# A new place in SBUF for the tiles of an MLP's second matrix, other pairs for the sums of its blocks, and one VectorE operation for the final scaling

## The chip, the cores and the metric

The kernel runs on one core of a Trainium2 chip. TensorE multiplies, VectorE, ScalarE and GpSimd work on vectors, and SyncE's queue issues nearly all DMA transfers. The metric is the device time of one execution in microseconds (us). An execution takes a little longer than the span of the profile, which runs from its first to its last instruction.

## The reference, cut to what matters

One step of a decoder layer for 1024 prompt tokens and 32 sample tokens (T = 1056 columns in all), with a width of 1024: attention and a short convolution, merged and projected, then an MLP and a last normalization. Everything is float32. The change touches the end alone:

```
h2 = rms_norm(x2, g_mlp)              # 1056 x 1024
u  = square(relu(h2 @ w_up))          # 1056 x 4096
x3 = x2 + u @ w_down                  # 1056 x 1024
y  = rms_norm(x3, g_final)
```

## The kernel before, in words

**Split products.** A float32 factor is split into a high part (a ScalarE cast to the matmul's reduced float32 type) and a low part (a VectorE subtraction), and each product is three matmuls (mm3: high by high, high by low, low by high; lines 216 to 218 of the profile). So each weight or activation tile costs a load, a cast and a subtraction before TensorE can use it.

**Strassen-like blocks.** Both matrix products of the MLP are cut into 2 x 2 blocks and done with seven block products in place of eight (Winograd's form). Each needs sums of blocks of the weights and of the activations.

**The stage of w_up** runs over 16 pairs p of column blocks of w_up. A pair is seven products, numbered 1 to 7 here: product 1 with hA[0], 2 with hA[1], then those with t2, t3, t1, t4 and b22, which are sums of blocks of h2. One product is 24 matmuls into one wide PSUM buffer (tile c); there are four such buffers. VectorE adds each product to what it belongs to, ScalarE applies the square of relu (put, line 1473), and SyncE stores the result u to DRAM (u_d, line 1478).

**The sums of w_down.** Between these products, VectorE also makes the sums of w_down's blocks, 16 blocks in all: load_sums loads two 512 KB pieces into a slot of tile h2r (line 1485), sums_down adds four times (lines 1492 to 1495) and stores 1 MB to DRAM (sd_d, line 1496). SDOWN says in which pair which block is done: block p - 1 in pair p, and blocks 14 and 15 both in pair 15. A pair's first block is put behind product 5, a second one behind product 7. There are four slots of h2r; three of them hold low parts of t1, t4 and b22 during the pairs, so one is free for the sums. Block 15 takes the slot of t1's low part, once product 5 of pair 15 has been done.

**The stage of w_down.** For n in (1, 2, 5, 6, 7, 4) it runs over 16 values of p. Each p takes a tile of activations (u_of: for n = 1 the tiles T0 to T15 are loaded from u_d, line 1567, and stay, since later n need them; for n = 2 tiles ur are loaded), and a weight block of 128 x 512 (wrd, line 1552, from w_down itself or from sd_d). Casts (lines 1554 for the weights, 1560 for the activations) and subtractions (1555 and 1561) make the split tiles whd and ud. Then come 96 matmuls into four PSUM buffers, one for each of four column blocks d. At the end of an n the four buffers are copied or added into accumulators acc. The product n = 3 follows, with calls of rows_out in it that finish rows which are complete, and a tail with the remaining rows (rows_out for row tiles 8, 6, 7; last for 4 and 5).

**The final scaling.** rows_out squares a row tile on ScalarE, adds on VectorE, takes the power -1/2 on GpSimd (factor, line 1670), and multiplies by that factor and by g_final: for the row tiles that start at the rows in YV with one VectorE operation (line 1683), for the others with ScalarE (1685) and then GpSimd (1686).

**Where tiles lie.** Pools are opened from the left and from the right end of SBUF. When the pools of w_up's stage close ("hB", "q", "w", "h2"), those of w_down's stage take their room, in the order in which they are opened. A new tile waits for the last readers of the old tiles under it (reuse_waits="tile"). Before, from the left, in bytes of a partition: ud [18112, 35008), where hA[0] was and a little of hA[1]; wd (the split weights) [35008, 51392), the rest of hA[1]; T [51392, 85184), over all four h2r slots, with T0 at the top, over the slot of b22's low part, which product 7 reads.

**The order.** The order of instructions on each engine and queue is set ahead of the run by the framework's scheduler, which plays the program through with estimates of its own (schedule_with_timeline_sim=True). On the chip each engine and queue goes through its list in that order and stops at an instruction whose semaphores aren't there yet.

Of the kernel before, what the change touches and what calls it, by code (L numbers as in the profile page):

```python
# [11 lines left out]
F32 = mybir.dt.float32  # L12
# [4 lines left out]
OP = mybir.AluOpType  # L17
# [8 lines left out]
T = SEQ + NB * ST  # L26
HC = T // 2
# [41 lines left out]
UG = 1  # L69
TORDER = (0, 1, 2, 3, 8, 4, 5, 6, 7)  # L70
NP0 = 4
SDOWN = {**{p: (p - 1,) for p in range(1, 15)}, 15: (14, 15)}
WUB = 6
YV = (384, 512)
CB = 2
SADV = [2] * 10
SSTEP = [0, 0, 0, 0, 0, 0, 6, 6, 6, 6, 6, 6, 6, 6, 6, 7]
# [46 lines left out]
def tile_hybrid_step(ctx, tc, xp, xs, cck, ccv, csk, csv, swk, swv, sconv, ptab, g_attn, w_in,  # L124
# [5 lines left out]
    PE, V, S, P, DMA = nc.tensor, nc.vector, nc.scalar, nc.gpsimd, nc.sync  # L130
# [3 lines left out]
    def open_pool(name, side, bufs=1, **kw):  # L134
        es = ExitStack()
        pools[name] = es
        kw.setdefault("reuse_waits", "tile")
        return es.enter_context(tc.tile_pool(name=name, bufs=bufs, side=side, **kw))

    def close(*names):  # L140
        for n in names:
            pools.pop(n).close()

    cp = open_pool("cp", "left")
# [47 lines left out]
    def tok_rows(tt):  # L192
        if tt < 8:
            return xp[0, tt * 128:(tt + 1) * 128, :], 128
        return xs.rearrange("b t d -> (b t) d"), 32
# [19 lines left out]
    def mm3(out, wh, wl, ah, al, first, last):  # L215
        PE.matmul(out, wh, ah, start=first, stop=False)  # L216
        PE.matmul(out, wh, al, start=False, stop=False)  # L217
        PE.matmul(out, wl, ah, start=False, stop=last)  # L218
# [44 lines left out]
    for tt in range(9):  # L263
        src, m = tok_rows(tt)
        xt = wp.tile([128, D], F32, name="wru", tag="wru", bufs=WB)
# [8 lines left out]
        rs = ap_.tile([128, 1], F32, name="rs", tag="rs")  # L274
# [41 lines left out]
    for br, (c0, n, kc) in enumerate(((C_KC, 384, 256), (C_VS, 408, 128))):  # L316
        whs = [load_qkv(c0, n, k, P) for k in range(KT)] if br else wq
        h9 = h9 if br else pack(qp, hTh, hTl, "h9")
        for tt in range(9):
# [9 lines left out]
            m = 128 if tt < 8 else 32  # L329
# [90 lines left out]
    for j in range(4):  # L420
# [9 lines left out]
        for e in range(2):  # L430
# [3 lines left out]
                            op0=OP.mult)  # L434
# [307 lines left out]
    class Unit:  # L742
# [54 lines left out]
        def factor(self, br, parts=1):  # L797
            if parts == 2:
                V.tensor_add(self.st[:, br, 2, :], self.st[:, br, 2, :], self.st[:, br, 3, :])
            V.reciprocal(self.st[:, br, 3, :], self.st[:, br, 2, :])  # L800
# [168 lines left out]
    for j in range(16):  # L969
        js = slice(j % 8 * 128, j % 8 * 128 + 128)  # L970
        c = (C_GA, C_GB)[j // 8] + j % 8 * 128
# [30 lines left out]
    up = open_pool("unit", "right", bufs=2)  # L1002
# [400 lines left out]
    def wide():  # L1403
        return bank["p"].tile([128, 2, 512], F32, name="c", tag="c", bufs=bank["tags"]["c"])
# [14 lines left out]
    def load_up(f):  # L1419
        raw = wp.tile([128, KT, 128], F32, name="wru", tag="wru", bufs=4)  # L1420
        DMA.dma_start(raw, w_up[0, :, f * 128:(f + 1) * 128].rearrange("(k p) c -> p k c", p=128))
        return raw[:, :4], raw[:, 4:]

    def halves(raw):
        h, l = (wp.tile([128, 4, 128], F32R, name="wu" + x, tag="wu" + x, bufs=WUB) for x in "hl")
        S.copy(h, raw)
        V.tensor_sub(l, raw, f32(h))
        return h, l

    def product(w, h):  # L1430

        c = wide()[:, :, :HC // 2]
        for k in range(4):
            for i in range(2):
                s = slice(i * HC // 2, (i + 1) * HC // 2)
                mm3(c[:, i], w[0][:, k], w[1][:, k], h[0][:, k, s], h[1][:, k, s], k == 0, k == 3)
        return c
# [42 lines left out]
    def load_sums(p):  # L1480

        w = h2p.tile([128, 4, HC], F32, name="h2r", tag="h2r", bufs=4)
        w = w.rearrange("p a b -> p (a b)")[:, :2 * D].rearrange("p (a b) -> p a b", a=2)
        for i in range(2):
            DMA.dma_start(w[:, i], w_dn[0, (p + 16 * i) * 128:(p + 16 * i + 1) * 128])
        return p, w
# [11 lines left out]
    for p in range(16):  # L1498
        sd = [load_sums(i) for i in SDOWN.get(p, ())]
        w11, w12 = load_up(p)  # L1500
# [19 lines left out]
        c = product(halves(s1), hB["t1"])  # L1520
# [16 lines left out]

    up = open_pool("ud", "left")  # L1540
    dp = open_pool("wd", "left")
    rp = open_pool("T", "left")
    wp = open_pool("w", "right")
    lp = open_pool("mlp", "right")
    accp = open_pool("acc", "right")
    accs = [accp.tile([128, 4, HC], F32, name=f"acc{i}") for i in range(4)]
    res = [rp.tile([128, HC], F32, name=f"T{p}") for p in reversed(range(16))][::-1]
    lows = [None] * 3

    def split_w(src, pool=dp, tag="whd", bufs=4):  # L1550
        raw = wp.tile([128, 512], F32, name="wrd", tag="wrd", bufs=4)
        DMA.dma_start(raw, src)
        h, l = (pool.tile([128, 512], F32R, name="whd", tag=tag + x, bufs=bufs) for x in "hl")
        S.copy(h, raw)  # L1554
        lows.append(V.tensor_sub(l, raw, f32(h)))  # L1555
        return h, l

    def split_u(raw, c0=0, c1=HC, pool=up, tag="ud", bufs=4):
        h, l = (pool.tile([128, c1 - c0], F32R, name="ud", tag=tag + x, bufs=bufs) for x in "hl")
        S.copy(h, raw[:, c0:c1])  # L1560
        V.tensor_sub(l, raw[:, c0:c1], f32(h))
        return h, l
# [10 lines left out]
    def u_of(n, p):  # L1573

        if n == 1:
            return load_u(p, 0, res[p])
        if n == 2:
            return load_u(p + 16, 0)
        raw = load_u(*{5: (p, 1), 6: (p + 16, 1), 7: (p, 0), 4: (p + 16, 0), 3: (p + 16, 1)}[n])
        if n != 3:  # L1580

            with tc.issue_after(lows[-2].ins):
                if n in (5, 6):
                    V.tensor_sub(res[p], raw, res[p])
                    return res[p]
                V.tensor_sub(raw, res[p], raw)
        return raw

    def w_of(n, p):
        return {1: down_w(0, p)[:, :512], 2: down_w(1, p)[:, :512], 4: down_w(1, p)[:, 512:], 5: sd_d[p, :, 1, 512:],  # L1590
                6: sd_d[p, :, 0, :512], 7: sd_d[p, :, 0, 512:], 3: sd_d[p, :, 1, :512]}[n]
# [3 lines left out]
    for n in (1, 2, 5, 6, 7, 4):  # L1595
        cs = [wide()[:, :, :HC // 2] for _ in range(4)]
        for p in range(16):
            u = u_of(n, p)
            wh, wl = split_w(w_of(n, p))
            uh, ul = split_u(u)  # L1600
            if n == 2:

                ws.append(split_w(w_of(3, p), lp, "w3", 16))
            for d in range(4):
                ds = slice(d * 128, d * 128 + 128)
                for i in range(2):
                    s = slice(i * HC // 2, (i + 1) * HC // 2)
                    mm3(cs[d][:, i], wh[:, ds], wl[:, ds], uh[:, s], ul[:, s], p == 0, p == 15)
            if p >= 4 and behind:
                V.tensor_add(*behind.pop(0))  # L1610
        for d, c in enumerate(cs):
            a0, a1, a2, a3 = (a[:, d].rearrange("p (i c) -> p i c", i=2) for a in accs)
            if n == 1:
                S.copy(a0, c)
            elif n == 2:
                V.tensor_add(a1, c, a0)
            elif n == 5:
                S.copy(a2, c)
            elif n == 4:
                V.tensor_sub(a0, a0, c)  # L1620
            else:
                V.tensor_add(a0, c, a0)
            if n in (6, 7):
                behind.append((a3 if n == 6 else a2, a0, a2))
    close("T", "wd")

# [2 lines left out]
    gf = op.tile([128, D], F32, name="gf", bufs=1)  # L1631
# [29 lines left out]
    def sums(n):  # L1661

        ss = op.tile([128, n + 1], F32, name=f"ss{n}", tag=f"ss{n}")
        P.memset(ss[:, n:], D * EPS)
        return ss
# [7 lines left out]
    def rows_out(tt):  # L1673
        t0, m = tt * 128, 128 if tt < 8 else 32
        xt = residual(tt)
        yt = op.tile([128, D], F32, name="yt", tag="yt")
        ss = sums(2)
        for q in range(2):
            h = slice(q * 512, q * 512 + 512)
            S.activation(yt[:m, h], xt[:m, h], AF.Square, accum_out=ss[:m, q:q + 1])  # L1680
        rs = factor(ss, m)
        if t0 in YV:
            V.scalar_tensor_tensor(yt[:m], xt[:m], rs[:m], gf[:m], op0=OP.mult, op1=OP.mult)
        else:
            S.mul(yt[:m], xt[:m], rs[:m])
            P.tensor_mul(yt[:m], yt[:m], gf[:m])
        DMA.dma_start(y_p[0, t0:t0 + m, :] if t0 < SEQ else y_s.rearrange("b t d -> (b t) d"), yt[:m])


# [35 lines left out]
    for tt in (8, 6, 7):  # L1725
        rows_out(tt)
    last(5, early[1])
    bank["e"].close()
    close("out", "ud", "acc", "mlp", "w", "cp")
_INS = ["x_prompt", "x_sample", "cache_cmp_k", "cache_cmp_v", "cache_slc_k", "cache_slc_v", "state_win_k",  # L1730
        "state_win_v", "state_conv", "page_table", "g_attn", "w_in", "cmp_pe_k", "cmp_w1_k", "cmp_w2_k",
        "cmp_pe_v", "cmp_w1_v", "cmp_w2_v", "conv_w", "conv_b", "w_nsa_out", "w_conv_out", "w_o", "g_mlp",
# [29 lines left out]
```

## Time and profile before

| | us |
|---|---|
| median of 3 runs | 1980.15 (1978.64 to 1980.93) |
| the profiled execution | 1979.56 |
| its span | 1977.8 |
| TensorE busy | 1917.4 |
| last product of w_up's stage ends | 1610.98 |
| first matmul of w_down's stage | 1626.40 |
| last two stores issued | 1973.83 to 1974.79 |

The profiled execution lies 0.6 us below the median, within the spread of the runs. Its mean granted TensorE clock is 0.987 of full speed. In the profile's lines, L1567 is line 1567 of the kernel, "c<-ud,whd" is the tile written and the tiles read, SPq is SyncE's queue of DMA issues, and PE, DVE, ACT and POOL are TensorE, VectorE, ScalarE and GpSimd. PEld is TensorE's loading of weights. "<-" behind an idle time names what ended it.

### The profile page before, as it was taken

The page shows a single profiled execution, that of the slowest core. Times are in us where ns is not written, and L with a number is a line of the kernel's source. Part 1 is how long each engine was busy: PE and PEld are TensorE (multiplying, and loading weights), DVE is VectorE, ACT ScalarE, POOL GpSimd, SP SyncE. Part 2 cuts the span into 40 slices and gives each one's busy share as a digit, 9 for nine tenths or more (in the row PEclk, how much of TensorE's full clock was granted, in tenths as well). Part 3 has the DMA queues.
Part 4 walks back from the last instruction along what each step waited for, and adds up shares of the span by engine and source line. Part 5 has one row for each costly group of instructions (what it writes and reads, how often), then busy time and mean ns, then how long its engine had stood idle before and what let it go on. Part 6 is the DMA issues. An engine that isn't in the chain of part 4 may idle for free.

```text
span 1977.8 us, 35184 instructions
## 1 busy us (share of the span) xinstructions
PE 1917.4 (97%) x13412; PEld 1784.6 (90%) x13412; DVE 1070.7 (54%) x2255; ACT 831.5 (42%) x1849; POOL 463.7 (23%) x640
## 2 busy tenths in 40 slices
PE   9999999999999999989999999999999969999998
PEld 8999999999998988877879887789999969999997
DVE  6324232545446777654633352597767644667755
ACT  5213233555456566533322131455545434443344
POOL 3112223434434544343223350120000000000003
PEclk9999999999999999989999999999999989999999
DMA  6365316222236430175535353537665564755654
GB/s 209 124 167 133 93 55 171 67 69 71 64 91 213 158 110 28 47 251 174 173 107 190 119 192 130 152 113 260 213 216 203 195 251 169 251 184 165 190 178 159
DMA packets 236249, 301.70 MB, mean 153 GB/s; under 512 B 20597, under 2 KB 163078, under 8 KB 231984
## 3 DMA queue, kind: packets, MB, share of 16 engines
q1 hardware_dynamic: 229168, 265.89, 42.9%
q0 software_dynamic: 6912, 33.56, 5.0%
q8 instruction: 106, 1.74, 0.4%
q14 instruction: 63, 0.52, 0.1%
HBM read 220.68 MB, written 78.71 MB: 151 GB/s over the span
## 4 chain that ended last, share of the span: by engine, by line
PE 84%; DMA 7%; DVE 3%; ACT 2%; issue 2%; SPq 1%; POOL 1%; DVEq 0%; POOLq 0%; ACTq 0%
PE c L217 10%; PE c L216 10%; PE c L218 10%; PE PT L878 3%; PE ga L217 3%; PE ga L216 3%; PE ga L218 3%; PE hid L216 3%; PE hid L217 3%; PE hid L218 3%; PE pv L885 2%; PE pv L884 2%; PE sl L1131 2%; PE ct L498 1%; PE so L1170 1%
## 5 line engine op out<-in xcount | busy, mean ns | idle before, releaser
L216 PE MATMUL c<-ud,whd 128*128 128x264 f32 x768 | 218.4, 287 | 17.7 <-ACT ud L1560 15.4
L217 PE MATMUL c<-ud,whd 128*128 128x264 f32 x768 | 219.2, 286 | 0.0
L218 PE MATMUL c<-ud,whd 128*128 128x264 f32 x768 | 218.6, 286 | 0.0
L804 POOL TENSOR_SCALAR P<-P,st,gates 128x256 f32<-128x256 f32 (+4 forms) x272 | 150.6, 570 | 127.1 <-DVE st L800 94.8
L216 PEld LDWEIGHTS c<-ud,whd 128*128 128x128 f32 x768 | 145.7, 191 | 18.1 <-ACT ud L1560 15.7
L216 PE MATMUL hid<-cth,w1h 128*128 128x254 f32 x512 | 148.7, 291 | 4.7 <-ACT cth L513 4.6
L217 PE MATMUL hid<-ctl,w1h 128*128 128x254 f32 x512 | 150.2, 293 | 0.0
L216 PE MATMUL c<-hBt,wuh 128*128 128x264 f32 x512 | 145.1, 283 | 1.1 <-ACT p L1444 1.1
L217 PEld LDWEIGHTS c<-ud,whd 128*128 128x128 f32 x768 | 146.1, 190 | 0.0
L218 PE MATMUL hid<-cth,w1l 128*128 128x254 f32 x512 | 146.0, 285 | 0.0
L218 PEld LDWEIGHTS c<-ud,whd 128*128 128x128 f32 x768 | 145.4, 190 | 0.0
L218 PE MATMUL c<-hBt,wul 128*128 128x264 f32 x512 | 145.3, 284 | 0.0
L1554 ACT CAST whd<-wrd 128x512 fp32r<-128x512 f32 x112 | 68.6, 622 | 158.1 <-issue 105.0
L882 DVE TENSOR_TENSOR ptl<-PT,pth 128x512 fp32r<-128x512 f32 (+1 forms) x148 | 99.5, 685 | 65.4 <-ACT pth L881 65.0
L216 PE MATMUL ga<-hTh,whu 128*128 128x384 f32 (+1 forms) x384 | 128.2, 334 | 0.0
L239 POOL TENSOR_TENSOR wlu<-wru,whu 128x1024 fp32r<-128x1024 f32 x32 | 76.7, 2398 | 215.4 <-ACT whu L238 215.4
L1555 DVE TENSOR_TENSOR whd<-wrd,whd 128x512 fp32r<-128x512 f32 x112 | 76.4, 691 | 93.6 <-ACT whd L1554 93.5
L217 PE MATMUL ga<-hTl,whu 128*128 128x384 f32 (+1 forms) x384 | 126.7, 330 | 0.0
L218 PE MATMUL ga<-hTh,wlu 128*128 128x384 f32 (+1 forms) x384 | 126.2, 329 | 0.0
L217 PE MATMUL c<-h2r,wuh 128*128 128x264 f32 x384 | 109.9, 286 | 1.9 <-DVE h2r L1470 1.0
L881 ACT CAST pth<-PT 128x512 fp32r<-128x512 f32 (+1 forms) x148 | 83.8, 588 | 66.2 <-PE PT L878 63.1
L216 PEld LDWEIGHTS hid<-cth,w1h 128*128 128x128 f32 x512 | 98.2, 192 | 9.1 <-ACT cth L513 6.9
(518 smaller groups left out, 5817.5 us busy)
## 6 DMA issues: line engine op xcount, KB each, us to landing
ur<-u_d SPq DMA_DIRECT2D x96, 264.0 KB
wru<-in_w_up SPq DMA_DIRECT2D x36, 512.0 KB
u_d<-u SPq DMA_DIRECT2D x64, 264.0 KB
wru<-in_w_in SPq DMA_DIRECT2D x32, 512.0 KB
h2r<-in_w_down SPq DMA_DIRECT2D x32, 512.0 KB
sd_d<-h2r SPq DMA_DIRECT2D x16, 1024.0 KB
wrd<-sd_d SPq DMA_DIRECT2D x64, 256.0 KB
wrd<-in_w_down SPq DMA_DIRECT2D x48, 256.0 KB
```

The costliest lines, as they stand in the source:

```text
L216: PE.matmul(out, wh, ah, start=first, stop=False)
L217: PE.matmul(out, wh, al, start=False, stop=False)
L218: PE.matmul(out, wl, ah, start=False, stop=last)
L239: (leng or P.tensor_sub)(l, raw, f32(h))
L804: P.tensor_scalar(p, p, self.st[:, br, 3, g:g + 1], gates[:, self.qi, 3 * hg + br:3 * hg + br + 1], op0=OP.mult, op1=OP.mult)
L878: PE.transpose(pt[:n, g * 128:(g + 1) * 128], pg[g], ident)
L881: S.copy(hi[:n], pt[:n])
L882: V.tensor_sub(lo[:n], pt[:n], f32(hi[:n]))
L884: PE.matmul(self.o, w, hi[:n], start=first and i == 0, stop=False)
L885: PE.matmul(self.o, w, lo[:n], start=False, stop=last and i == len(tiles) - 1)
L1554: S.copy(h, raw)
L1555: lows.append(V.tensor_sub(l, raw, f32(h)))
```

## The change

Four things change:

- SDOWN: pairs 1 to 10 do one block of sums each, as before; pairs 11, 12 and 13 do two each (10 and 11, 12 and 13, 14 and 15); pairs 14 and 15 do none.
- The pools of w_down's stage are opened in another order: from the left T first, then wd; ud moves to the right end. The tiles of T are now laid out upwards from T0. T takes the 33,792 bytes of hA, exactly; wd lies over h2r's first two slots (t4's low part and the slot of the sums), and ud over room of the pool that held the split weights of w_up.
- The four copies of the sums of n = 1 into acc go from ScalarE to VectorE.
- The final scaling of rows_out is one VectorE operation for every row tile.

```diff
-SDOWN = {**{p: (p - 1,) for p in range(1, 15)}, 15: (14, 15)}
+SDOWN = {**{p: (p - 1,) for p in range(1, 11)}, 11: (10, 11), 12: (12, 13), 13: (14, 15)}
 WUB = 6
-YV = (384, 512)
...
-    up = open_pool("ud", "left")
+
+    rp = open_pool("T", "left")
     dp = open_pool("wd", "left")
-    rp = open_pool("T", "left")
     wp = open_pool("w", "right")
+    up = open_pool("ud", "right")
     lp = open_pool("mlp", "right")
     accp = open_pool("acc", "right")
     accs = [accp.tile([128, 4, HC], F32, name=f"acc{i}") for i in range(4)]
-    res = [rp.tile([128, HC], F32, name=f"T{p}") for p in reversed(range(16))][::-1]
+    res = [rp.tile([128, HC], F32, name=f"T{p}") for p in range(16)]
...
             if n == 1:
-                S.copy(a0, c)
+                V.tensor_copy(a0, c)
...
-    close("T", "wd")
+    close("wd", "T")
...
         rs = factor(ss, m)
-        if t0 in YV:
-            V.scalar_tensor_tensor(yt[:m], xt[:m], rs[:m], gf[:m], op0=OP.mult, op1=OP.mult)
-        else:
-            S.mul(yt[:m], xt[:m], rs[:m])
-            P.tensor_mul(yt[:m], yt[:m], gf[:m])
+        V.scalar_tensor_tensor(yt[:m], xt[:m], rs[:m], gf[:m], op0=OP.mult, op1=OP.mult)
...
-    close("out", "ud", "acc", "mlp", "w", "cp")
+    close("out", "acc", "mlp", "ud", "w", "cp")
```

## The prediction

> **What bounds the kernel now.** I read the page's busy times first, then the waits of TensorE over the last stages, then the chain of waits through the longest of them, and then the timelines of the engines that it names.
>
> ```profile
> span 1977.8 us, 35184 instructions
> PE 1917.4 (97%) x13412; PEld 1784.6 (90%) x13412; DVE 1070.7 (54%) x2255; ACT 831.5 (42%) x1849; POOL 463.7 (23%) x640
> ```
>
> TensorE is busy 97% of the span, so only its idle time can be won, 60 us in all, and what slows its clock. From 1400 us to the end, its waits are these (engine, tile, line, releaser: total us, times, longest):
>
> ```profile
> PE c L216 <- ACT ud L1560: 15.4, 1, 15.4
> PE c L216 <- ACT acc L1614: 2.2, 1, 2.2
> PE dn L216 <- ACT ud L1560: 0.5, 1, 0.5
> PE dn L216 <- DVE acc L1620: 0.4, 1, 0.4
> PE dn L217 <- DVE ud L1561: 0.3, 1, 0.3
> ```
>
> One wait of 15.4 us stands between the stage of w_up and that of w_down, one of 2.2 us between the products n = 1 and n = 2. The chain of waits through the first, and SyncE's timeline:
>
> ```profile
> 1610.85 0.13 PE c L218
> ...
> 1619.10 6.60 DMA T<-u_d
> ...
> 1625.72 0.64 ACT ud L1560
> ...
> 1626.40 1.25 PE c L216 x4
> ```
>
> ```profile
> 1607.26 0.33 SPq L1478 DMA_DIRECT2D u_d<-u  x1
> 1610.15 0.33 SPq L1496 DMA_DIRECT2D sd_d<-h2r  x1
> 1610.58 0.37 SPq L1478 DMA_DIRECT2D u_d<-u  x1
> 1610.99 3.29 SPq L1552 DMA_DIRECT2D wrd<-in_w_down  x4
> 1614.38 0.41 SPq L1478 DMA_DIRECT2D u_d<-u  x1
> 1614.89 0.38 SPq L1496 DMA_DIRECT2D sd_d<-h2r  x1
> 1615.36 3.70 SPq L1567 DMA_DIRECT2D ur<-u_d  x4
> 1619.10 4.23 SPq L1567 DMA_DIRECT2D T<-u_d  x5
> ```
>
> The products of w_up end at 1610.98. T0, the first tile that n = 1 multiplies, is only asked for at 1619.10, behind four weight blocks, the last stores and even the four ur tiles of n = 2, because T0 lay over a slot still in use. It lands 6.60 us later. Over this stretch the transfers, not SyncE alone, are full (columns: stretch, length, PE, PEld, DVE, ACT, POOL busy, TensorE's granted clock, DMA share, GB/s):
>
> ```profile
> 1611.00:1626.40 15.40, 0.00 (x0) 0.00 (x0) 6.11 (x10) 4.39 (x8) 0.00 (x0) 0.66 1.01 371
> 1626.40:1629.60 3.20, 3.20 (x14) 3.20 (x15) 2.72 (x4) 1.89 (x3) 0.00 (x0) 0.50 1.05 400
> 1677.00:1680.70 3.70, 3.70 (x18) 3.70 (x19) 2.04 (x4) 2.98 (x6) 0.00 (x0) 0.56 0.45 158
> 1533.00:1553.00 20.00, 20.00 (x168) 20.00 (x167) 13.87 (x22) 9.66 (x16) 0.00 (x0) 1.00 0.60 206
> ```
>
> After the stall TensorE runs 3.2 us at clock 0.50, so it loses half of them, 1.6 us; after the gap of 2.2 us it runs 3.7 us at 0.56, which loses 1.6 us too.
>
> **The change, part by part.** *The layout.* T now lies over hA, which products 1 and 2 of pair 15 read last, and the split weights over two h2r slots. So T0 needn't wait for a slot that late stores hold. When will it be issued? Not necessarily under the last pair: the wrd tiles lay over a weight buffer last read by product 5 of the last pair's seven (of 20/7 = 2.9 us each by the row at 1533, so until about 1605.2), and SyncE was free from 1607.59 to 1610.15, yet they were issued at 1610.99, right behind TensorE's last product. I take from this that the written order keeps a new pool behind all readers of the pool whose room it takes, though the waits go by tile. Then T0 comes right behind the store of product 6. That store stands at 1610.58 behind a 0.43 us sd_d issue that moves away, so T0 is asked for at about 1610.5 and wrd0, next in the program, at about 1610.9. What does a load take when the queues are not crowded? In the next stretch:
>
> ```profile
> 1658.55 3.04 DMA wrd<-sd_d
> ```
>
> T0 lands at 1613.6 by that, wrd0 at 1613.9 to 1614.3. Their casts on ScalarE (0.64 us each, the row above at 1625.72) end at 1614.9, and TensorE starts at 1615.0: a stall of 4.0 us. The bounds: with no crowding and T0 issued behind the previous store, 3.4; with wrd0 as late as before, 6.0, from this row of ScalarE (16.34 + 0.62 − 10.98):
>
> ```profile
> 1616.34 0.62 ACT L1554 CAST whd<-wrd 128x512 fp32r<-128x512 f32 x1 [3.27 <-DMA wrd<-in_w_down]
> ```
>
> I take 4.0, since the two 1 MB stores that ran beside that load are gone. Gain 15.4 − 4.0 = 11.4 (9.4 to 12.0). The slow stretch behind it stays in the sum: the 2.2 us gap brings one as well. The Trainium skill, "TensorE: Matmul & The Clock Gate", section "What's actually happening", has the clock fall to half after at least one idle window of about 3.4 us; the row at 1677.00 shows it after 2.2 us, so trace and page differ. By the page, a stall of 3.4 us or less would keep the clock, and the sum would be 1.6 us lower.
>
> *The sums.* Blocks 10 to 15 now fall two to a pair into pairs 11 to 13. Work is neither added nor removed: four VectorE sums, two loads of 512 KB and a 1 MB store per block. An ordinary pair has VectorE busy 13.87 of 20 us and DMA at 0.60 (the row at 1533); one more block adds four sums of 0.68 us, 2.7 us, to make 16.6 of 20, and 2 MB, 2.1 MB / 20 us = 105 GB/s on 206. What hides it is a TensorE that is busy throughout; the cover breaks only when VectorE stands still (the last rival). Cost 0, from 0 to 5 us (below).
>
> *The copy of the sums of n = 1* goes from ScalarE to VectorE.
>
> ```profile
> 1675.79 0.62 ACT L1554 CAST whd<-wrd 128x512 fp32r<-128x512 f32 x1 [2.39 <-DMA wrd<-sd_d]
> 1676.32 1.59 ACT L1614 COPY acc<-c 128x528 f32<-128x528 f32 x3
> ```
>
> ```profile
> 1673.75 0.70 DVE L1561 TENSOR_TENSOR ud<-ur,ud 128x528 fp32r<-128x528 f32 x1
> 1676.44 0.69 DVE L1555 TENSOR_TENSOR whd<-wrd,whd 128x512 fp32r<-128x512 f32 x1 [1.99 <-ACT whd L1554]
> ```
>
> On ScalarE the copies stood behind a cast that waited for a load; TensorE, whose four buffers were all taken, waited for the first copy. VectorE is free from 1674.45 to 1676.44. If the copies stand ahead of the subtraction at 1676.44, stall and slow stretch go: 2.2 + 1.6 = 3.8. If behind it, they start at 1677.13, 0.8 later than before, a loss of 1. An order that leaves a short gap gives between; I take 2.2, nearer the first, since VectorE needs the cast of the same block to end first and so stands later in any order.
>
> *The final scaling* becomes one VectorE operation in the six calls of rows_out that used a ScalarE and a GpSimd one; the seventh already had it.
>
> ```profile
> L1686 POOL TENSOR_TENSOR yt<-yt,gf 128x1024 f32<-128x1024 f32 (+1 forms) x6 | 14.3, 2387 | 8.5 <-ACT yt L1685 8.5
> L1683 DVE SCALAR_TENSOR_TENSOR yt<-x,rs,gf 128x1024 f32<-128x1024 f32 x1 | 1.3, 1285 | 0.5 <-POOL ss L1664 0.5
> ```
>
> ```profile
> 1970.13 2.34 POOL L1686 TENSOR_TENSOR yt<-yt,gf 128x1024 f32<-128x1024 f32 x1 [1.26 <-ACT yt L1685]
> 1972.43 0.55 POOL L1670 TENSOR_TENSOR rs<-rs,nhalf 128x1 f32<-128x1 f32 x1
> ```
>
> ```profile
> 1968.91 0.42 DVE L1717 TENSOR_TENSOR x<-dn,x 128x256 f32<-128x256 f32 x1 [1.53 <-PE dn L218]
> 1970.56 0.16 DVE L1669 TENSOR_REDUCE rs<-ss 128x1 f32<-128x4 f32 x1 [1.23 <-ACT ye L1718]
> 1973.02 1.42 DVE L1721 SCALAR_TENSOR_TENSOR ye<-x,rs,gf 128x512 f32<-128x512 f32 x2 [2.30 <-POOL rs L1670]
> ```
>
> At the very end the power for the last rows (1972.43) stood behind GpSimd's multiplication of the rows before. Without it: last addition done by about 1969.5 (1969.33, or a little later behind a 1.29 us scaling), its square about 1970.0, reduction 1970.1, power 1970.2 to 1970.75, scaling at 1970.8 in place of 1973.02. Gain 2.2 (1.5 if the scaling holds the addition up, 2.5 if not); the last stores follow as before. During n = 3, VectorE takes three scalings of 1.29 us; TensorE's three waits there (dn, above) total 1.2 us, so the effect lies between −0.8 (one scaling in the way, less the 0.5 us of idle time in front of the one that is there now) and +0.6, half of those waits; I take 0.3, the wait on a VectorE subtraction, which GpSimd no longer works beside.
>
> **The sum.** 11.4 + 2.2 + 2.2 + 0.3 = 16.1. The profiled execution took 1979.56 us, 1.76 beyond its span, and the median is 1980.15, 0.6 above it; so 1963.5 as profiled, 1964.0 by the median.
>
> **The rivals.**
> *Full hiding.* T0 and wrd0 are asked for under the last pair, since by tile nothing holds them. For it: hA is last read by product 2, five products before the end, so it is free from about 1596.5. Against: the wrd row above. The stall goes with its slow stretch: 15.4 + 1.6 + 2.2 + 2.2 + 0.3 = 21.7, so 1958.4 (1956 to 1961).
> *The loads crowd each other.* T tiles and weight blocks are all asked for at once, and each goes as slowly as T0 did, 6.60 us: start at 1610.5 + 6.6 + 0.7 = 1617.8, a stall of 6.8 and a sum 2.8 smaller, 1966.8. For it: 371 GB/s at a share of 1.01; against: 2 MB of stores are gone from the stretch.
> *The change doesn't do what it says.* The order still puts T0 behind the ur tiles, or the split weights wait for block 15's store in the slot that they now lie over; the stall stays at 15.4, the copies stand behind the subtraction, and only the tail is left: 2.2 − 1 = 1.2, so 1979.0. For it: the order was written by estimates that I can't see. Against: nothing lies over T any more.
> *Slower: VectorE stands at the second block's sums.* These lines are a block's store, the next block's load and the last addition of that pair:
>
> ```profile
> 1549.71 0.32 SPq L1496 DMA_DIRECT2D sd_d<-h2r  x1
> 1554.55 0.88 SPq L1485 DMA_DIRECT2D h2r<-in_w_down  x2
> ```
>
> ```profile
> 1550.15 0.70 DVE L1531 TENSOR_TENSOR x<-c,u 128x528 f32<-128x528 f32 x1
> ```
>
> With one slot free, a second block is loaded only 4.8 us behind the first one's store; if its sums stand right behind the pair's last addition on VectorE (the L1531 row, which ends 1.1 us behind that store), VectorE waits 4.8 + 3 to 6.6 − 1.1 = 7 to 10 us, and all additions from PSUM stand behind it. TensorE has four buffers and needs 2.9 us for each, so it goes on for three more, 8.7 us. At 10 us it loses 1.3 in each of three pairs, 4 to 5 us in all; if VectorE stands for the whole round of a block (4.8 + 6.6 + 2.7 for its sums + about 2 to the store = 16), it loses 7.3 × 3 = 22, so 1986. The change is slower from a loss of 16 on, 5.4 a pair, which is VectorE standing 14 us. Against: the sums of before stood in VectorE's order where their data was there.
>
> **Chances.** Forecast 0.60 (its own range 1961 to 1971, the bounds summed), full hiding 0.17, crowding 0.12, no effect 0.06, slower 0.05. About 0.2%, 4 us, is what a measurement here tells from no change. Faster than 1976.2 are the first three, less a little for a loss in the pairs: 0.88; the same 0.06; slower 0.06. The range, 1956.5 to 1973, holds the first three cases.
>
> **What would show it.** The layout: T and wrd issued within 1 us of the last product, behind product 6's store, and a wait of about 4 us on ud L1560, then clock 0.5 again; T issued before 1608 would show full hiding, landings over 5 us crowding. The copies: no 2.2 us wait on acc. The tail: GpSimd's power within 0.3 us of the reduction. The sums: TensorE without idle time in pairs 11 to 14; waits there on VectorE would make me wrong, and so would a stall of over 7 us.

## The result and the profile after

The changed kernel takes 1965.7 us (median of 6 runs, 1963.79 to 1968.18), beside 1980.54 us for the kernel before (6 runs). The ratio is 0.9925, with a 95% interval of 0.9911 to 0.9938: about 15 us faster, where 16.1 had been forecast. The profiled execution took 1968.18 us, which is the slowest of the six. Its page begins with

```profile
span 1966.3 us, 35170 instructions
```

and TensorE's waits from 1400 us to the end (who waits, for which tile, on which line; who ended the wait: total us, times, longest) are now

```profile
PE c L215 <- ACT whd L1554: 4.1, 1, 4.1
PE c L215 <- DVE acc L1616: 2.5, 1, 2.5
PE c L216 <- DVE ud L1561: 1.0, 1, 1.0
PE dn L215 <- DVE acc L1620: 0.4, 1, 0.4
```

The 15.4 us in front of n = 1 have become 4.1, and the 2.2 us in front of n = 2 are gone. But two waits are new, of 1.0 and 2.5 us: they lie at the end of n = 2. No wait stands in pairs 11 to 14. SyncE's timeline at the change of stages, and ScalarE's:

```profile
1597.77 0.32 SPq L1495 DMA_DIRECT2D sd_d<-h2r  x1
1599.74 10.84 SPq L1477 DMA_DIRECT2D u_d<-u  x3
1610.62 0.43 SPq L1567 DMA_DIRECT2D T<-u_d  x1
1611.39 0.33 SPq L1552 DMA_DIRECT2D wrd<-in_w_down  x1
```

```profile
1613.90 0.63 ACT L1560 CAST ud<-T 128x528 fp32r<-128x528 f32 x1 [0.75 <-DMA T<-u_d]
1614.48 0.62 ACT L1554 CAST whd<-wrd 128x512 fp32r<-128x512 f32 x1
```

The last block of sums is stored at 1597.77, T0 is asked for right behind the store of product 6, its cast starts 3.3 us later, and TensorE starts at 1615.15. On the chip the six blocks of pairs 11 to 13 don't run two to a pair: one slot serves them, and their stores are issued 12.5 to 16.0 us apart (1529.43, 1545.42, 1559.21, 1572.43, 1585.26 and 1597.77), while a pair takes 20.4 us. So the last one falls into pair 15, which begins at 1590.53. The window behind TensorE's start (stretch, length, the five engines' busy time and instructions, granted clock, DMA share, GB/s) shows half the clock:

```profile
1615.15:1619.80 4.65, 4.64 (x21) 4.65 (x22) 2.77 (x5) 2.44 (x4) 0.00 (x0) 0.50 0.95 335
```

Stage by stage, the profiled executions compare as follows. The columns are the wait between the last product of w_up and n = 1; the time from the first matmul of one n to the first of the next; n = 3 with everything up to TensorE's last matmul; the tail behind that; and the sum of it all, n = 6, 7 and 4 included (about 140.1 to 140.2 in each). Each number is a difference of two times in TensorE's timeline, where a stage n is 384 matmuls: 24 for each of the 16 values of p, and 96 in all for each of the four buffers. The rows e1 to e12 are the kernels of the experiments.

| kernel | wait | n = 1 | n = 2 | n = 5 | n = 3 | tail | sum |
|---|---|---|---|---|---|---|---|
| before | 15.44 | 50.56 | 48.26 | 46.69 | 56.84 | 8.91 | 366.81 |
| changed | 4.11 | 48.91 | 50.82 | 48.37 | 55.39 | 7.47 | 355.27 |
| changed, again (e10) | 4.44 | 48.42 | 49.02 | 46.78 | 55.34 | 6.69 | 350.89 |
| e1, copies on ScalarE | 4.29 | 50.77 | 48.37 | 46.76 | 55.34 | 6.68 | 352.40 |
| e2, six wrd buffers | 4.52 | 49.26 | 47.97 | 46.79 | 55.34 | 6.69 | 350.75 |
| e3, sums as before | 15.77 | 48.70 | 49.32 | 46.79 | 55.34 | 6.68 | 362.79 |
| e4, scaling alone | 15.66 | 51.24 | 48.28 | 46.70 | 55.92 | 6.68 | 364.58 |
| e5, sums alone | 4.42 | 51.72 | 47.85 | 46.77 | 56.74 | 8.55 | 356.15 |
| e6, p = 0 and 1 early | 0 | 56.74 | 49.64 | 48.21 | 55.38 | 6.69 | 356.70 |
| e7, early, six wrd | 0 | 56.53 | 47.20 | 46.79 | 55.38 | 6.68 | 352.63 |
| e8, early, six wrd, w3 spread | 0 | 57.11 | 51.67 | 49.60 | 55.37 | 6.68 | 360.50 |
| e9, sums and scaling | 4.46 | 50.61 | 48.27 | 46.70 | 56.01 | 7.15 | 353.30 |
| e11, early in another pool, six wrd | 0 | 51.51 | 47.44 | 46.78 | 55.37 | 6.68 | 347.84 |
| e12, additions first | 4.16 | 48.21 | 47.73 | 46.82 | 55.34 | 6.68 | 349.14 |

A stage n without any wait and at full clock takes 46.7 us (n = 5 to 4 of most rows). What is above that is wait or slow clock.

### The profile page after: what moved, and what is told of

Same layout as the page of the kernel before. It is cut to its first block, busy times and chain, and to the rows that moved or that the text cites. A ratio compares the mean times of both kernels' runs of the same rounds, so it can differ in the third digit from the quotient of the medians.

```text
span 1966.3 us, 35170 instructions
## 1 busy us (share of the span) xinstructions
PE 1914.1 (97%) x13412; PEld 1780.9 (91%) x13412; DVE 1076.4 (55%) x2265; ACT 822.6 (42%) x1839; POOL 448.7 (23%) x634
```

## The experiments

### Which part of the change took away the 11 us: layout or sums?

The prediction gave that gain to the layout and nothing to the sums. Two kernels take them apart.

**e3** is the changed kernel with the sums where they were:

```diff
-SDOWN = {**{p: (p - 1,) for p in range(1, 11)}, 11: (10, 11), 12: (12, 13), 13: (14, 15)}
+SDOWN = {**{p: (p - 1,) for p in range(1, 15)}, 15: (14, 15)}
```

> The changed kernel with the sums of the blocks back in the pairs that they had before (14 and 15 in pair 15); layout, copies and scaling as changed. If the layout alone brings the gain in front of n = 1, the wait there stays near 4 us and the time is the changed kernel's within 1 us. If moving the sums is needed too, the two 1 MB stores lie between the loads again, and the split weights wait for the slot of the sums: a wait of 7 to 12 us, and 3 to 8 us longer than the changed kernel.

Measured: 0.9994 of the kernel before (0.9982 to 1.0007), so no gain can be told any more. The interval still admits the 3 us that the scaling brings (e4), and the profile is 4.0 us shorter than that of the kernel before from the end of w_up's products on. The wait of 15.8 us is longer than the 7 to 12 us that were expected for this case, and the loss larger than 3 to 8 us. TensorE's longest wait, and SyncE's timeline behind the end of w_up's products at 1607.12:

```profile
PE c L215 <- ACT ud L1560: 15.8, 1, 15.8
```

```profile
1607.15 3.32 SPq L1552 DMA_DIRECT2D wrd<-in_w_down  x4
1610.57 0.42 SPq L1477 DMA_DIRECT2D u_d<-u  x1
1611.09 0.38 SPq L1495 DMA_DIRECT2D sd_d<-h2r  x1
1611.52 4.39 SPq L1567 DMA_DIRECT2D ur<-u_d  x4
1615.95 3.83 SPq L1567 DMA_DIRECT2D T<-u_d  x5
```

It is the order of the kernel before, issue for issue. T0 now lies over hA, which product 2 read last, some 14 us earlier; still its load stands behind block 15's store and the four ur tiles. No tile under T0 needed that store. T's pool, however, lies over the pool that holds hA and the h2r slots, and that store is the last reader of this pool. That this holds T back is a conclusion so far; e5, e6 and e11 test it.

**e5** is the kernel before, with the new SDOWN and nothing else (the line of the diff above, the other way round).

> The kernel before with the sums of the blocks alone moved to the pairs of the change; layout, copies and scaling as before. Theory F (T is held back by the order, which keeps it behind the last reader of the whole pool of hA and h2r; that was block 15's store, and with the sums gone it is product 7 whatever the layout): T0 is asked for within 1 us of the last product, the wait in front of n = 1 falls from 15.4 to 4 to 6 us, and the time is 9.5 to 11.5 us below the kernel before. Theory G (the new layout is needed, since T0 lay over a slot that product 7 reads and others over slots of the sums): the wait stays above 8 us and the gain is under 7 us.

Measured: 0.9947 (0.9929 to 0.9966), 10.5 us faster, with these waits and this timeline (products of w_up end at 1609.16):

```profile
PE c L216 <- ACT whd L1554: 4.4, 1, 4.4
PE c L216 <- ACT acc L1614: 2.2, 1, 2.2
PE c L216 <- DVE acc L1616: 0.9, 1, 0.9
...
```

```profile
1609.07 0.32 SPq L1567 DMA_DIRECT2D T<-u_d  x1
1609.72 0.33 SPq L1552 DMA_DIRECT2D wrd<-in_w_down  x1
```

In the old layout, too, T0 is asked for at the end of the last product. So the sums' move alone makes this gain, and the layout alone makes none of it. Theory F holds in all its figures, theory G falls.

### The final scaling by itself

**e4** is the kernel before with `if t0 in YV:` made `if True:`.

> The kernel before with the final scaling alone changed to one VectorE operation; layout, sums and copies as before. Theory D (the tail and the gain within n = 3 both come from the scaling): from TensorE's last matmul to the end about 7.5 us in place of 8.9, n = 3 and its tail of matmuls about 55.4 in place of 56.8, together 2.9 us faster than before. Theory E (n = 3 gained by the new layout or order): the tail falls by 1.4, n = 3 stays at 56.8, 1.4 us faster.

Measured: 0.9985 (0.9974 to 0.9996), about 3.0 us faster. GpSimd and VectorE at the end:

```profile
1968.54 0.55 POOL L1670 TENSOR_TENSOR rs<-rs,nhalf 128x1 f32<-128x1 f32 x1 [3.23 <-DVE rs L1669]
```

```profile
1968.24 0.16 DVE L1669 TENSOR_REDUCE rs<-ss 128x1 f32<-128x4 f32 x1 [0.57 <-ACT ye L1718]
1969.12 1.41 DVE L1721 SCALAR_TENSOR_TENSOR ye<-x,rs,gf 128x512 f32<-128x512 f32 x2 [0.73 <-POOL rs L1670]
```

The power starts 0.3 us behind the start of its reduction, and the tail is 6.68 us in place of 8.91, 2.2 less, not the 1.4 that was expected from the changed kernel's profile. n = 3 falls by 0.9 (56.84 to 55.92). That is between theories D and E. The remaining 0.5 to 0.6 us of n = 3 go with the new layout (55.34 to 55.39 in every kernel that has it, 55.92 and 56.01 in e4 and e9, which have not); why was not tested.

### Both of these, without the layout and the copies

**e9** is the kernel before with the edits of e5 and e4. **e10** is the changed kernel once more, measured beside e9.

> The kernel before with the sums moved and the final scaling on VectorE; layout and copies as before. If layout and copies bring nothing of their own, its time is that of the changed kernel of this comparison within 1.5 us, some 13 to 15 us below the kernel before, with a wait of about 4.4 in front of n = 1, one of 2.2 on acc in front of n = 2, and a tail of 6.7 us. If they do, it is 2 us or more slower than the changed kernel.

> The changed kernel once more, beside the others of this comparison. If the waits of 1.0 and 2.5 us at the end of n = 2 and the tail of 7.5 us belong to it, they are there again within 0.5 us each; the tail, which hung on one store that took 4.1 us, is more likely 6.7, as in all the other kernels with this scaling. Time 13 to 16 us below the kernel before.

Measured: e9 0.9929 (0.9916 to 0.9943), e10 0.9937 (0.9923 to 0.9950). No difference can be told: layout and copies bring nothing that these times show, though the intervals would hide some 4 us either way. Both medians lie 12.3 and 12.6 us below the kernel before, a little less than the 13 that were expected at least. In its profile e10 is 2.4 us shorter from the end of w_up's products on (the table), which the medians (1964.25 and 1963.99) don't bear out. Its waits:

```profile
PE c L215 <- ACT whd L1554: 4.4, 1, 4.4
PE c L215 <- DVE acc L1616: 2.1, 1, 2.1
...
```

The wait on acc is there again; the one on ud is not, and the tail is 6.69. So the 1.0 us and 0.8 us of the longer tail belong to the first profile. In that one, ScalarE waited at the end for an earlier store to leave one of the two buffers of yt:

```profile
1955.83 0.63 ACT L1680 ACTIVATE yt<-x 128x512 f32<-128x512 f32 x1 [4.32 <-DMA out<-yt]
```

so that the scaling of row tile 7 came late on VectorE and held up the last addition. e9 has such a wait too (4.28 us there, tail 7.15).

### The copies, and the wait at the end of n = 2

**e1** puts the four copies of the sums of n = 1 back:

```diff
-                V.tensor_copy(a0, c)
+                S.copy(a0, c)
```

> The changed kernel with the four copies of n = 1 put back on ScalarE; all else as changed. Theory A (n = 2 is bound by the round trip of its loads, and a gap before it is time in which the loads catch up): the gap of about 2.2 us in front of n = 2 and its slow stretch come back, and the new waits at the end of n = 2 (1.0 on ud and 2.5 on acc) shrink to under 1 us in all; the time is that of the changed kernel within 1.5 us. Theory B (the copies are worth their 3.8 us, the waits at the end of n = 2 have nothing to do with them): the gap comes back, the waits at the end of n = 2 stay, and the time is 3 to 4 us longer than the changed kernel's.

Measured: 0.9933 (0.9917 to 0.9950).

```profile
PE c L215 <- ACT whd L1554: 4.3, 1, 4.3
PE c L215 <- ACT acc L1614: 2.2, 1, 2.2
...
```

The 2.2 us in front of n = 2 come back and the waits at its end go, as theory A has it and theory B doesn't. No difference in time from the changed kernel can be told (0.9925, and 0.9937 in e10), but the intervals are too wide to rule out the 3 us of theory B by the time alone. Nor are the copies the only cause of a wait at the end of n = 2: e5 has them on ScalarE and still waits 0.9 us on acc there. n = 1, 2 and 5 together take 145.9 us here, 148.1 and 144.2 in the two profiles of the changed kernel: the copies are worth between 1.7 us won and 2.2 us lost.

**e2** gives wrd six buffers:

```diff
-        raw = wp.tile([128, 512], F32, name="wrd", tag="wrd", bufs=4)
+        raw = wp.tile([128, 512], F32, name="wrd", tag="wrd", bufs=6)
```

> The changed kernel with six buffers for wrd in place of four; all else as changed. Theory A (the loads of n = 2 turn round too slowly through four buffers): loads are asked for earlier, the waits of 1.0 and 2.5 us at the end of n = 2 go, and the slow stretch behind them too: n = 2 and n = 5 take about 47 us each in place of 50.8 and 48.4, so the profiled time falls by 4 to 5 us and the median by 2 to 5. Theory C (the waits come from VectorE's order: the addition into acc stands behind subtractions that are due later): no change within 1 us.

Measured: 0.9916 (0.9899 to 0.9932), median 1960.59.

```profile
PE c L215 <- ACT whd L1554: 4.5, 1, 4.5
PE c L215 <- DVE acc L1616: 1.0, 1, 1.0
...
```

The wait on acc falls to 1.0 but doesn't go, and the interval overlaps the changed kernel's. That is less than theory A asked for.

**e12** leaves the four buffers and changes VectorE's order. What makes T for p = 2 to 5 of n = 5 is held back until the last of the four additions at the end of n = 2 has been issued:

```diff
-                V.tensor_add(a1, c, a0)
+                added.append(V.tensor_add(a1, c, a0))
...
-            with tc.issue_after(lows[-2].ins):
+            with tc.issue_after((added[3] if n == 5 and p in (2, 3, 4, 5) else lows[-2]).ins):
```

> The changed kernel, with the subtractions that make T for p = 2 to 5 of n = 5 held back, in the order on VectorE, until the four additions into acc at the end of n = 2 have been issued; four buffers for wrd and all else as changed. Theory C (the wait at the end of n = 2 comes from VectorE's order, in which the additions stand behind work of the next product): the wait on acc of 2.1 to 2.5 us falls under 0.8, and n = 2 and n = 5 together take 94.5 to 96 us in place of 95.8 to 99.2; the time falls by 1 to 3 us. Theory A (what is late are the loads of n = 2, and the order only passes it on): the wait stays, on acc or on a tile of n = 2, within 0.7 us of what it was, or comes back at the first p of n = 5.

Measured: 0.9913 (0.9898 to 0.9928), median 1960.91. First VectorE in the changed kernel, then in e12, with e12's waits:

```profile
1706.08 0.69 DVE L1555 TENSOR_TENSOR whd<-wrd,whd 128x512 fp32r<-128x512 f32 x1 [3.36 <-ACT whd L1554]
...
1713.43 0.70 DVE L1584 TENSOR_TENSOR T<-ur,T 128x528 f32<-128x528 f32 x1
1714.05 0.70 DVE L1616 TENSOR_TENSOR acc<-c,acc 128x528 f32<-128x528 f32 x1
```

```profile
1706.16 0.69 DVE L1555 TENSOR_TENSOR whd<-wrd,whd 128x512 fp32r<-128x512 f32 x1
1706.77 2.54 DVE L1617 TENSOR_TENSOR acc<-c,acc 128x528 f32<-128x528 f32 x4
1709.23 2.55 DVE L1584 TENSOR_TENSOR T<-ur,T 128x528 f32<-128x528 f32 x4
```

```profile
PE c L215 <- ACT whd L1554: 4.9, 2, 4.2
PE dn L215 <- DVE acc L1621: 0.4, 1, 0.4
```

In the changed kernel VectorE stood for 3.36 us for a late weight block and then worked without a break, but had thirteen operations in front of the first addition (1706.08 to 1713.43), most of them for n = 5. With the additions first, no wait on acc is left; 0.7 us come back at the first p of n = 5 (the second of the two waits on whd). n = 2 and n = 5 take 94.55 us in place of 99.2 and 95.8. So theory C explains the larger part: the wait was made by the place of the additions in VectorE's order. What theory A has is the start of it, a load that is late; e2 shows that more buffers make it smaller.

### Hiding the last 4 us

**e6** loads T0, T1 and the first two weight blocks in pair 15 and splits them there, in free buffers of w_up's pools; T0 and T1 are loaded into their own places at the end of n = 1. The core of its edit:

```diff
+        if p == 15:
+            early_w = wp.tile([128, KT, 128], F32, name="wru", tag="wru", bufs=4)
+            early_u = [part("p1", NP0) for _ in range(2)]
...
+                wh, wl = (z.rearrange("p a b -> p (a b)") for z in halves(early_w[:, 4 * j:4 * j + 4]))
...
+            if n == 1 and p < 2:
+                wh, wl, uh, ul = first[p]
```

> The changed kernel, with the activations and weights of p = 0 and 1 of n = 1 loaded during pair 15 into free buffers of w_up's stage and split there; T0 and T1 are loaded into their places at the end of n = 1. Nothing is left out. Theory H (the wait of 4.1 us is the time from the first request to TensorE, and the slow clock follows from it): the wait in front of n = 1 falls under 1 us, the granted clock stays at 1.0, p = 2 is ready after 5.8 us, and the time is 3.5 to 6 us below the changed kernel's. Theory I (the loads behind are the limit): a wait of 2 to 5 us appears at p = 2 or 3, or the waits at the end of n = 2 grow by as much, and less than 2 us is left.

Measured: 0.9945 (0.9926 to 0.9965), no gain over the changed kernel.

```profile
PE c L215 <- ACT whd L1570: 7.7, 1, 7.7
```

```profile
1605.54 2.30 SPq L1583 DMA_DIRECT2D T<-u_d  x5
1608.04 0.32 SPq L1477 DMA_DIRECT2D u_d<-u  x1
1608.41 3.85 SPq L1583 DMA_DIRECT2D T<-u_d  x6
1613.39 2.30 SPq L1568 DMA_DIRECT2D wrd<-in_w_down  x4
```

The products of w_up end at 1605.91 and p = 0 and 1 follow without a gap at full clock, as theory H has it; then TensorE waits 7.7 us at p = 2, more than the 2 to 5 us of theory I. The weight blocks wrd for it are asked for at 1613.39, behind eleven loads of T. They lie over w_up's weight pool, and the early split weights are in that pool, so its last reader is now p = 1 (to 1611.8). By the tiles nothing holds them back: in bytes of a partition wrd takes [221152, 229344), where the low part for product 5 and three sums of weight blocks lay, while the early split weights lie at [200672, 204768) and [212960, 217056). That wrd stands so late in the order would follow from the same rule that kept T behind block 15's store in e3; e11 tests it.

**e7** adds six wrd buffers to e6; **e8** also loads every second w3 block in n = 5 in place of n = 2 (`if n in (2, 5) and p % 2 == 0`).

> The early p = 0 and 1 of n = 1 together with six buffers for wrd. If the two limits are separate, the gains add: 3.5 to 6 us from the first, 2 to 5 from the second, so 1956 to 1960 us where the changed kernel has 1965.7. If the first gain is only lent by the loads of n = 2, six buffers keep more of it than four do, and the time is that of six buffers alone within 1 us.

> As the kernel with both, and the 16 weight blocks of n = 3 are loaded half in n = 2 and half in n = 5, where all came in n = 2. If the loads of n = 2 are still a limit with six buffers, what is left of waits at its end goes (1.0 us with its short slow stretch) and the time falls by 1 to 2 us; if not, it stays within 0.5 us, and waits of n = 5 would show the loads moved to a place that can't carry them.

Measured: e7 0.9939 (0.9918 to 0.9959), with nearly the same wait, 7.5 us, at p = 2; the gains don't add, nor does the time come within 1 us of that of six buffers alone (0.9916 in e2; the two intervals overlap). e8 0.9962 (0.9950 to 0.9974), slower (its fastest run, 1969.35, lies above e7's slowest, 1966.54): a wait of 4.8 us on acc at the end of n = 2, though fewer loads fall into it. VectorE stands there for an ur load of n = 5, with the additions behind it:

```profile
1712.76 0.71 DVE L1600 TENSOR_TENSOR T<-ur,T 128x528 f32<-128x528 f32 x1 [1.40 <-DMA ur<-u_d]
...
1715.83 0.70 DVE L1638 TENSOR_TENSOR acc<-c,acc 128x528 f32<-128x528 f32 x1
```

which is what e12 then tested.

**e11** keeps the early split tiles out of the weight pool: they lie in the pool q, over which only later tiles come; six wrd buffers as in e7.

```diff
-                wh, wl = (z.rearrange("p a b -> p (a b)") for z in halves(early_w[:, 4 * j:4 * j + 4]))
+                uh, wh, wl = (qp.tile([128, 2, HC // 2], F32R, name=t, tag=t, bufs={"e": 3}.get(t, NP0))
+                              .rearrange("p i c -> p (i c)") for t in tags)
```

> Six buffers for wrd, and p = 0 and 1 of n = 1 loaded and split in pair 15 as in the earlier kernel of that kind, but with their split tiles in the pool of w_up's stage over which only late tiles lie (q), not in the pool of its weights (w), over which wrd lies. Nothing is left out. If a new pool stands behind the last reader of the old one in the order, the blocks wrd for p = 2 are now asked for behind product 7 and not behind p = 1: T2 and wrd2 by 1613.5 on a scale on which w_up's products end at 1611, p = 2 ready about when p = 1 ends, a wait of 0 to 1.5 us there in place of 7.5, and 3 to 6 us less time than with six buffers alone, so 18 to 22 us below the kernel before. If the wait at p = 2 comes from full queues instead, it stays above 4 us.

Measured: 0.9910 (0.9897 to 0.9924). The median is 1958.83 us, 17.7 below the kernel before (18 to 22 were expected), where the changed kernel, measured beside it (e10), has 1963.99; the slowest of its five runs (1961.18) is below the fastest of e10's (1962.16).

```profile
PE c L215 <- ACT whd L1572: 3.0, 1, 3.0
```

```profile
1608.19 2.30 SPq L1585 DMA_DIRECT2D T<-u_d  x5
1610.59 0.38 SPq L1570 DMA_DIRECT2D wrd<-in_w_down  x1
```

```profile
1616.75 0.62 ACT L1572 CAST whd<-wrd 128x512 fp32r<-128x512 f32 x1 [1.38 <-DMA wrd<-in_w_down]
```

On a scale on which w_up's products end at 1611, wrd for p = 2 is asked for at 1613.0, where in e6 it was 1618.5, as the rule of the pools has it. The wait at p = 2 is 3.0 us, twice what was expected: the block took 6.2 us from its request to its cast (1610.59 to 1616.75), behind five loads of T, with the transfers at a share of 0.95 and 326 GB/s meanwhile. So a part of that wait is likely a crowded queue. This kernel is faster than both that the case began with. How much of that the early loads bring isn't shown: against e2 (six buffers alone) or e12 the times tell nothing (0.9916 and 0.9913, measured at other times), and e11 and e12 were not run together in one kernel.

## Why the prediction was right, and where it was wrong

**The time and the main term.** 1964.0 was forecast and 1965.7 measured. The wait in front of n = 1 was put at 4.0 us and is 4.1 (4.4 in e10); T0 was to be asked for at 1610.5 and is at 1610.62; its cast was to end at about 1614.9 together with wrd's, and wrd's ends at 1615.1. Of the two casts wrd's comes last, so the wait is put down to whd and not to ud, which the prediction's sign named. The slow clock behind it stays, as forecast, but for longer than the 3.2 us of the kernel before: 0.50 over 4.65 us, a loss of 2.3 us in place of 1.6. The aside that a stall of 3.4 us or less would make the sum 1.6 us lower can mean the time alone, for a full clock adds to the gain; the stall was longer in any case. Full hiding did not happen, and crowding did not at this place.

**The cause of the main term was wrong.** The step "The layout ... So T0 needn't wait for a slot that late stores hold" gave 11.4 us to the layout, and the step on the sums gave them "Cost 0, from 0 to 5 us". e3 and e5 show the reverse. The mistake lies within the prediction itself: it took from the early weight blocks that a new pool stands behind all readers of the pool whose room it takes, and used that, rightly, for the place of T0 in the changed kernel, but not for the kernel before. There it explained T0's late load by the slot under the tile, where block 15's store, the last reader of T's whole old pool, held it back. By that rule T is set free by the move of the sums, in either layout. That the wrong cause cost nothing is luck: the two edits were made together, so the sum was right all the same.

**The sums' other side** was right in its result: no wait of TensorE in pairs 11 to 14. The mechanism of the slower rival is there, though small. VectorE does stand at a block's first addition for its load, which the kernel before doesn't show:

```profile
DVE h2r L1491 <- DMA h2r<-in_w_down: 9.8, 5, 3.0
```

These are five waits from 1490 us to the end of w_up's products, of 3.0 us at most, where the rival put 7 to 10, and TensorE's four buffers cover them. The 16.6 us of VectorE in 20 were worked out for two blocks in a pair; spread as they are, the blocks load it less.

**The copies** were valued at 2.2. The gap did go (n = 1 falls by 1.65 us in the profile), but the step took the gap's length as won and did not ask what is late next: VectorE's additions at the end of n = 2 were, and cost 2.1 to 2.5 us, in one profile 1.0 more and a slow stretch. In its place stands e1: no difference that the times can tell.

**The tail** was right at 2.2 (e4, e10); the changed kernel's first profile shows 1.4, by a wait for a buffer of yt that was not foreseen. **n = 3** was undersized: 0.3 forecast, 0.9 from the scaling (e4) and 1.45 in all. So the copies were put too high and n = 3 too low, and the two misses partly cancel in the sum.

In the first profile the terms are 11.3 for the wait, 1.65 for n = 1, −2.6 for n = 2, −1.7 for n = 5, 1.45 for n = 3 and 1.45 for the tail: 11.5 us with the rest. That execution is the slowest of six; e10's profile, the shortest of its five, has 15.9 by the same count.

## What to carry to other kernels

Where an order is written ahead by pools, look up the last reader of the whole old pool, not of the tile that lies under the new one: e3 and e6 lost 11 and 7 us to a store and a product that no tile under theirs needed, and e5 won 10.5 by moving work out of the last pairs. A gap that is removed from an engine is worth its length only if what comes next is on time; follow the queue of the engine that serves it (here VectorE's) for one stage more. Two edits made together need an experiment for each before either is called the cause.

## What the runs showed that was not expected

**The clock after a gap.** A gap of two microseconds doesn't always slow TensorE's clock. The windows, with the columns as above, behind a gap of 2.52 us in the changed kernel, of 2.05 in e10, and of 2.34 in e3:

```profile
1714.90:1718.60 3.70, 3.70 (x19) 3.70 (x20) 3.70 (x7) 0.00 (x0) 0.00 (x0) 0.57 0.52 163
```

```profile
1711.40:1715.00 3.60, 3.60 (x30) 3.60 (x31) 3.60 (x7) 0.00 (x0) 0.00 (x0) 1.00 0.57 206
```

```profile
1720.95:1724.60 3.65, 3.65 (x30) 3.65 (x31) 3.65 (x7) 0.00 (x0) 0.00 (x0) 1.00 0.55 182
```

The kernel before had a slow stretch (0.56) behind 2.22 us, e5 none behind 2.23. So the length alone doesn't decide.

What fits is the place of the gap. Within each profile the changes of the granted clock lie whole multiples of 3.41 us apart, as if TensorE's activity were judged in windows of that length. With windows laid so, from the end of w_up's products on, half clock follows every window at full clock in which TensorE stood for 1.94 us or more, and none in which it stood for 1.79 us or less, in all 14 profiles. The gap of 2.22 us in the kernel before lies in one such window, the first of the next two rows (TensorE busy 1.19 of 3.41 us, and half clock behind it):

```profile
1674.02:1677.43 3.41, 1.19 (x10) 0.98 (x9) 1.12 (x2) 1.64 (x4) 0.00 (x0) 1.00 0.88 306
1677.43:1680.84 3.41, 3.41 (x18) 3.41 (x17) 2.00 (x3) 2.55 (x5) 0.00 (x0) 0.50 0.40 140
```

That of 2.05 us in e10 is shared between two, and the clock stays full:

```profile
1706.85:1710.27 3.42, 2.48 (x21) 2.27 (x19) 3.42 (x7) 2.08 (x5) 0.00 (x0) 1.00 0.91 322
1710.27:1713.68 3.41, 2.30 (x19) 2.33 (x20) 3.41 (x7) 0.18 (x1) 0.00 (x0) 1.00 0.90 332
```

The 2.23 us of e5 (0.70 and 1.53) and the 2.34 of e3 (0.67 and 1.67) are shared likewise. No run moves such a gap by itself, so this is read from the traces and not tested. The Trainium skill, "TensorE: Matmul & The Clock Gate", section "What's actually happening", says that the windows by which activity is judged run freely, whatever the kernel does; that agrees with these rows, while its rule that half clock comes after at least one idle window of about 3.4 us does not: the drop comes behind gaps of 2.2 to 2.5 us.

**A spread that lies ahead of the change.** The last product of w_up ended between 1605.91 and 1611.05 us in these profiles, in kernels whose code up to pair 10 is the same. This is more than most of the effects measured here, which is why the stages were compared and not only the spans. TensorE's idle time ahead of that point differs by 6.5 us between the profiles (30.2 to 36.7), and its busy time at half clock by 13.8 (11.8 to 25.6), so the spread lies in its waits and its clock; what makes these differ stays open.
